# Attention products of different row groups and column halves issued alternately, in separate PSUM banks, in a two-block network on one core

## The chip, the core and the metric

The kernel is one program on one NeuronCore of a Trainium2 chip. What is measured is the device time of one execution, from the first to the last instruction, in microseconds (us). The engines are named as in the profile: PE (TensorE, the matrix products), PEld (its weight loads), DVE (VectorE), ACT (ScalarE), POOL (GpSimd), and SP, whose queue issues the loads from DRAM.

## The reference, cut to what matters

There are 256 tokens of width 1024, all in float32. A first block has a mixer (a dilated attention of 8 heads of 64 beside a retention), a cross attention to a memory, and a mixture of 32 experts. A second block has two layers, each of feed-forward, mixer, feed-forward, and each mixer runs four attentions side by side and one output projection:

```python
def _token_mixers(h, w_in, ...):
    proj = h @ w_in
    a, b, c, d = jnp.split(proj, ...)
    o_a = _mixer_window(a, sink, slopes[:WIN_HEADS])        # 4 heads of 64, 2 key/value heads
    o_b = _mixer_mla(b, ...)                                # 4 heads of 96, values of 64
    o_c = _mixer_axial(c, ax_q_norm, ax_k_norm)             # 4 heads of 64, 2 key/value heads
    o_d = _mixer_diff(d, ...)                               # 4 heads, 2 maps each, of 32
    return jnp.concatenate([o_a, o_b, o_c, o_d], axis=-1) @ w_out

def _dense_attention(q, k, v, scale):
    s = jnp.einsum('bqhgd,bkhd->bhgqk', qi, k).astype(jnp.float32) * scale
    p = jax.nn.softmax(s, axis=-1)
    return jnp.einsum('bhgqk,bkhd->bqhgd', p.astype(v.dtype), v)
```

Scores, softmax over 256 keys and the product with the values are what the change touches. The sums are the same before and after it.

## The kernel before, in words

Every dense product is made exact by splitting both operands into a high and a low part (hi + lo) and issuing three products: hi by hi, hi by lo, lo by hi (`mm3`, lines 308 to 312, so these products all carry the lines L310, L311 and L312). The weights come in chunks of 1 MB through a ring of four tiles, ACT copies the high part (L279), DVE or POOL subtracts the low part (L283).

An attention works on a pair of maps at a time. `scores` (L482) issues six products into one PSUM bank of the tag "mm": 128 tokens by twice 256 keys. Their contraction is short: 64 partitions in the dilated attention and in `gqa` (which computes the axial mixer, called "a", and the window mixer, "w"), 32 in `att_diff` ("d"). Operands of different heads lie on different partitions: the slices in HALVES are rows 0 to 63 and 64 to 127, and `att_diff` has four slices of 32. `softmax` (L429) reads the bank (DVE L437 or L442 for the minimum, ACT L451 for the exponentials), `ptrans` transposes the probabilities in PSUM (L401) and copies them back (ACT L473), and `pv` (L476) multiplies them with the values. An output of `pv` has 64 columns of values, so it takes half of the 128 output partitions; the other head's output goes to the other half of the same bank. These products are plain float32, and each is two matmul instructions in the trace.

Before the change the heads of a pair of halves follow each other: all of half 0 (two token tiles of scores, two softmaxes, transposes, `pv`), then all of half 1. In `att_diff` and the dilated attention the second half's `pv` follows a whole round of scores later; in `gqa` and `att_mla` both column halves are outputs of one call's loop.

PSUM has eight banks, two for each of four tags: "mm" for scores (and the feed-forward's products), "tr" for transposes and `pv`, "a" and "b" for dense accumulators. Inside a mixer of block 2 the dense products use "a" alone, and "b" only serves the last transposes of `att_diff`; the output projection (`dense_sq`, L341) then takes both "a" (token tile 0) and "b" (token tile 1).

The order on each engine is fixed when the program is built: a scheduling pass lays out the instructions by their place in the source and by when their operands and tiles are expected to be free (`schedule_with_timeline_sim=True`), so dense products from further down are put between an attention's steps. Each engine then runs its list strictly in order. Where `pe_order` (L304) is used, the products inside keep the order in which they are written, while others may still come between them. In the mixer of block 2 the source order is MIXERS = "BCHaDdAmw": projections B, C, H, attention a, projection D, attention d, projection A, attentions m and w, then the output projection.

Of the kernel before, what the change touches and what calls it, by code (L numbers as in the profile page):

```python
# [9 lines left out]
F32 = mybir.dt.float32  # L10
# [16 lines left out]
# slots that the dense pools leave free, and those that memory()'s do  # L27
M_EARLY, M_MID = 6, 5

# projections (capitals; H: the heads of B) and attentions of the four mixers in the order of their issue  # L30
MIXERS = "BCHaDdAmw"
OUT = [k for k in MIXERS if k in "adwm"]
# the first gate and up tiles with tokens on partitions; the last down pairs with token tile 0 first, the norm of
# that tile after PLACE of the other's products
NAT, TAIL, PLACE = 2, 3, 4
# products of zeros that bring the tensor engine to its full clock while the first loads arrive
WARM = 18

# ------------------------------------------------------------------ host layout

def _nat(w):
    """[K, N] -> chunks [128, 4 k-tiles, <=512 columns], column groups outermost."""
# [9 lines left out]
def _sq(w, halves=(0, 1)):  # L52
    """[1024, 1024] -> chunks [128, 4 k-tiles, 512 columns], halves of k outermost."""
    n = _nat(w)
    return [n[2 * c + h] for h in halves for c in range(2)]


def _trans(w):
    """[1024, N] -> chunks [128, 2 column tiles, 8 k-tiles, 128 columns]."""
# [55 lines left out]
def _ffn_order():  # L115
    """Gate/up tiles and down pairs in the order of their use."""
# [55 lines left out]
def _pack_moe(i):  # L172
    """Per group of 4 experts: gate and up [k-tile][128, 4, 512], down [half][ff tile][128, 4, 512]."""
# [23 lines left out]
# ------------------------------------------------------------------ program  # L197

class Net:
# [18 lines left out]
    # ---- storage  # L218
# [3 lines left out]
    def turn(s, tags):  # L222
        """The tags of a list in turn."""
        tags.append(tags.pop(0))
        return tags[-1]

    def banks(s):
        """Four accumulators, [token tile][half]."""
# [5 lines left out]
    def bcast(s, pool, name, n, off=0, tag=None, bufs=None, after=None):  # L234
        """A DRAM vector on every partition."""
# [7 lines left out]
    def column(s, pool, name, n, off=0, rep=1):  # L243
        """A DRAM vector down the partitions, rep times."""
# [7 lines left out]
    # ---- weights  # L252
# [12 lines left out]
    def weight(s, width=CH, parts=2, pool=None, own=None, cuts=1):  # L265
        """The next chunk, in parts, each as exact hi + lo, in the ring's tiles, pool's or own."""
# [24 lines left out]
    def own(s, p, i):  # L291
        """Tiles of pool p for a chunk."""
        return [[p.tile([128, CH // 2], F32R, name="own", tag=f"own{j}{k}{i}") for k in range(2)] for j in range(2)]

    def issue_after(s, i, j):
        """i, of the same engine as j, is issued after j."""
# [3 lines left out]
    def plan(s, spec):  # L300
        """Which of the next weight parts get their lo on GpSimd (not d), and after which of the last two powers."""
# [5 lines left out]
    # ---- products  # L307
# [1293 lines left out]
```

## Time and profile before

| | |
|---|---|
| time, median of 3 runs | 1754.07 us (1753.56 to 1755.35) |
| span of the profiled execution | 1753.4 us; the page gives no other time for it, and this is 0.7 us below the median |
| instructions | 24984, of which PE 10070 products and as many weight loads |
| PE busy | 1579.9 us, 90% of the span |
| DVE, ACT, POOL busy | 839.4 us (48%), 657.0 us (37%), 286.9 us (16%) |
| mean granted TensorE clock | 0.941 of full speed |
| dilated attention of block 1 | about 54 to 94 us |
| experts | up to about 722 us |
| attentions of the two mixers of block 2 | about 953 to 1026 us and 1464 to 1537 us |

A busy share is a mean over stages that have different limits: from about 318 us to the end of the experts the chain that ends last runs through the loads, in the rest mostly through PE. What a change in one stage is worth has to be read in that stage. A bar of a matmul in the trace is longer than the step to the next one, because products are pipelined; the step from one start to the next is what it costs.

### The profile page before, as it was taken

Reading aid. Unit: us, or ns where it says so; the run is one execution under the profiler, and the core shown is the slowest. Engines: PE = TensorE matmul, PEld = TensorE weight load, DVE = VectorE, ACT = ScalarE, POOL = GpSimd, SP = SyncE. Lnnn points to the kernel's source line nnn. Section 1 sums busy time; section 2 is a strip of 40 time slices with the busy share of each in tenths; the row PEclk is TensorE's granted clock in tenths of the full one; section 3 lists DMA queues with packets and bytes.
Section 4 is the critical chain, followed back from the end, with each engine's and each line's share of the span. In section 5 each row is a group of like instructions: output and inputs, shape, how many; then the busy total and the mean of one; then the engine's idle time right before and its main releaser. Section 6 shows DMA issues by size and latency. Waiting matters only on the chain.

```text
span 1753.4 us, 24984 instructions
## 1 busy us (share of the span) xinstructions
PE 1579.9 (90%) x10070; PEld 1216.1 (69%) x10070; DVE 839.4 (48%) x1471; ACT 657.0 (37%) x1124; POOL 286.9 (16%) x253
## 2 busy tenths in 40 slices
PE   8999897877667767899999989999999999989998
PEld 6777784322211211599998769999999988779997
DVE  5657653100000000454477675556655667765555
ACT  4655441100000000344435745445444536734442
POOL 4223321100000000222224250000100032340000
PEclk9999998987878877999999989999999999989999
DMA  7444858999999999955554234556355634155552
GB/s 273 142 177 157 327 213 327 419 421 420 421 420 419 421 421 420 368 183 181 190 188 144 97 145 168 192 187 246 143 181 183 240 127 135 49 189 183 181 191 73
DMA packets 66186, 419.06 MB, mean 239 GB/s; under 512 B 10640, under 2 KB 12176, under 8 KB 18704
## 3 DMA queue, kind: packets, MB, share of 16 engines
q1 hardware_dynamic: 66064, 417.39, 62.8%
q8 instruction: 82, 1.34, 0.3%
q14 instruction: 40, 0.33, 0.1%
HBM read 416.32 MB, written 1.05 MB: 238 GB/s over the span
## 4 chain that ended last, share of the span: by engine, by line
PE 55%; DMA 23%; DVE 3%; POOL 1%; issue 1%; ACT 1%; DVEq 0%; SPq 0%; ACTq 0%; POOLq 0%
DMA mraw<-in_wm 23%; PE ps L310 17%; PE ps L312 17%; PE ps L311 17%; PE ps L401 1%; PE ps L480 1%; PE ps L950 1%; DVE xa L1169 1%; PE ps L970 0%; POOL rq L418 0%; PE ps L927 0%; DVE xl L392 0%; DVE lnst L1197 0%; DVE wl L283 0%; POOL ropet L1381 0%
## 5 line engine op out<-in xcount | busy, mean ns | idle before, releaser
L283 DVE TENSOR_TENSOR wl<-raw,wh 128x1024 fp32r<-128x1024 f32 (+2 forms) x314 | 389.3, 1250 | 302.0 <-ACT wh L279 301.1
L279 ACT ACTIVATE wh<-raw 128x1024 fp32r<-128x1024 f32 (+2 forms) x356 | 371.0, 1052 | 351.5 <-PE ps L311 181.1
L310 PE MATMUL ps<-xh,wh 128*128 128x256 f32 x1424 | 402.1, 282 | 3.4 <-ACT cv L1469 3.4
L312 PE MATMUL ps<-xh,wl 128*128 128x256 f32 x1424 | 401.4, 282 | 0.0
L311 PE MATMUL ps<-xl,wh 128*128 128x256 f32 x1424 | 401.0, 282 | 0.0
L310 PEld LDWEIGHTS ps<-xh,wh 128*128 128x128 f32 x1424 | 268.3, 188 | 6.6 <-ACT cv L1469 3.8
L311 PEld LDWEIGHTS ps<-xl,wh 128*128 128x128 f32 x1424 | 268.4, 189 | 1.4
L312 PEld LDWEIGHTS ps<-xh,wl 128*128 128x128 f32 x1424 | 268.4, 188 | 0.8
L950 PE MATMUL ps<-mraw,xg 128*32 128x512 f32 x1024 | 167.7, 758 | 77.4 <-DMA mraw<-in_wm 77.3
L312 PE MATMUL ps<-wh,xl 128*128 128x512 f32 (+3 forms) x520 | 190.1, 370 | 6.5 <-DVE xl L392 6.3
L310 PE MATMUL ps<-wh,xh 128*128 128x512 f32 (+3 forms) x520 | 190.5, 376 | 4.9 <-ACT xh L391 4.1
L311 PE MATMUL ps<-wl,xh 128*128 128x512 f32 (+3 forms) x520 | 191.9, 370 | 2.7 <-POOL wl L283 1.3
L950 PEld LDWEIGHTS ps<-mraw,xg 128*32 128x32 f32 x1024 | 25.6, 119 | 209.0 <-DMA mraw<-in_wm 173.0
L418 POOL TENSOR_TENSOR rq<-rv,mhalf 128x1 f32<-128x1 f32 (+4 forms) x46 | 46.9, 1020 | 728.1 <-DVE rv L416 720.4
L283 POOL TENSOR_TENSOR wl<-raw,wh 128x1024 fp32r<-128x1024 f32 x42 | 103.7, 2473 | 280.9 <-ACT wh L279 263.6
L956 DVE TENSOR_TENSOR mf<-ps,mf 128x512 f32<-128x512 f32 x8 | 5.5, 691 | 248.0 <-PE ps L950 244.1
L312 PEld LDWEIGHTS ps<-wh,xl 128*128 128x128 f32 x520 | 100.6, 194 | 23.2 <-DVE xl L392 10.4
L310 PEld LDWEIGHTS ps<-wh,xh 128*128 128x128 f32 x520 | 100.7, 195 | 22.7 <-ACT xh L391 7.6
L311 PEld LDWEIGHTS ps<-wl,xh 128*128 128x128 f32 x520 | 101.4, 195 | 18.4 <-POOL wl L283 3.4
L311 PE MATMUL ps<-wl,hf 128*128 128x512 f32 x256 | 100.1, 391 | 0.0
L312 PE MATMUL ps<-wh,hf 128*128 128x512 f32 x256 | 100.1, 391 | 0.0
L310 PE MATMUL ps<-wh,hf 128*128 128x512 f32 x256 | 98.2, 390 | 0.0
(357 smaller groups left out, 1981.0 us busy)
## 6 DMA issues: line engine op xcount, KB each, us to landing
mraw<-in_wm SPq DMA_DIRECT2D x191, 1024.0 KB, 19.9
raw<-in_wd SPq DMA_DIRECT2D x179, 1024.0 KB, 4.8
raw<-in_wd SPq DMA_DIRECT2D x8, 512.0 KB, 8.4
raw<-in_wd SPq DMA_DIRECT2D x4, 832.0 KB, 4.7
bc_ln_g<-in_ln_g SPq DMA_DIRECT2D x6, 512.0 KB, 5.7
bc_ln_b<-in_ln_b SPq DMA_DIRECT2D x6, 512.0 KB, 6.5
raw<-in_wd SPq DMA_DIRECT2D x4, 768.0 KB, 4.3
bias<-in_bias SPq DMA_DIRECT2D x4, 512.0 KB, 5.9
```

The source lines that it names most:

```text
L279: s.nc.scalar.activation(h[:, :n], rc, AF.Copy)
L283: i = eng.tensor_tensor(l[:, :n], rc, h[:, :n].bitcast(F32), op=OP.subtract)
L310: mm(out, lhsT=lh, rhs=rh, start=start, stop=False)
L311: mm(out, lhsT=lh, rhs=rl, start=False, stop=False)
L312: mm(out, lhsT=ll, rhs=rh, start=False, stop=stop)
L401: s.nc.tensor.transpose(ps[:, b * 128:b * 128 + 128], src[:, b * 128:b * 128 + 128], s.ident)
L418: s.last_pow = s.nc.gpsimd.tensor_tensor(q, r, s.mhalf[:, :n], op=OP.pow)
L480: s.nc.tensor.matmul(out, lhsT=v(j), rhs=pt[:, 2 * i + j], start=first and j == 0, stop=last and j == 1)
L950: nc.tensor.matmul(ps[32 * e:32 * e + 32], lhsT=xg[:, k, 32 * e:32 * e + 32], rhs=w[:, e * FF:e * FF + FF], start=k == 0, stop=k == NK - 1 ...
L956: nc.vector.tensor_tensor(f, gu[1], f, op=OP.mult)
L1169: nc.vector.scalar_tensor_tensor(z[:, cs], z[:, cs], mv[:, 0:1], g[:, cs], op0=OP.subtract, op1=OP.mult)
```

## The change

`scores` now takes several sets of operands, gives each its own bank, and issues the products of the sets in turn, one of each, in written order (`pe_order`). The sets are two in the dilated attention and `gqa` (both halves of 64 rows) and four in `att_diff` (all slices of 32 rows). `pv` takes pairs of outputs in the two column halves and alternates them in the same way. So both halves of a head pair go through scores, softmax, transposes and `pv` together. The second token tile of `gqa` and two of the four sets of `att_diff` take their banks from the tag "b". The dilated attention issues the loads of both halves' biases at the start of a group; they still share two buffers. `att_diff` copies its output of both halves to SBUF at once. Six instead of four probability tiles are kept (five instead of three in the dilated attention), for which two scratch tiles join the tag "by". The cross attention's products in `memory` are written out in place and stay as they were. Comments are removed throughout; those lines are left out here.

```diff
@@ -419,16 +419,16 @@
-    def softmax(s, pool, ps, bias=None, slope=(1.0, 1.0), sink=None, norm=True, bufs=4):
+    def softmax(s, pool, ps, bias=None, slope=(1.0, 1.0), sink=None, norm=True, bufs=6):
...
@@ -466,32 +466,41 @@
-    def pv(s, out, v, pt, i, first=True, last=True):
-        for j in range(NT):
-            s.nc.tensor.matmul(out, lhsT=v(j), rhs=pt[:, 2 * i + j], start=first and j == 0, stop=last and j == 1)
-
-    def scores(s, q, k):
-        ps = s.bank("mm")
-        for i in range(2):
-            s.mm3(ps[:, i * S:i * S + S], q(i, 0), q(i, 1), k(i, 0), k(i, 1), True, True)
-        return ps
-
+    def pv(s, products):
+        with s.pe_order():
+            for n, pair in enumerate(products):
+                for j in range(NT):
+                    for out, v, pt, i in pair:
+                        s.nc.tensor.matmul(out, lhsT=v(j), rhs=pt[:, 2 * i + j], start=n + j == 0,
+                                           stop=n == len(products) - 1 and j == 1)
+    def scores(s, maps, tags=("mm", "mm")):
+        banks = [s.bank(t) for t in tags[:len(maps)]]
+        with s.pe_order():
+            for i in range(2):
+                for a, b in ((0, 0), (0, 1), (1, 0)):
+                    for (q, k), ps in zip(maps, banks):
+                        s.nc.tensor.matmul(ps[:, i * S:i * S + S], lhsT=q(i, a), rhs=k(i, b), start=a + b == 0,
+                                           stop=a == 1)
+        return banks
...
@@ -590,19 +599,20 @@
+            bias = [p.tile([128, 2, 2, S], F32, name="bias", tag="bias", bufs=2) for _ in HALVES]
+            for e in range(2):
+                nc.sync.dma_start(bias[e], a["bias1"][:, 4 * g + 2 * e:4 * g + 2 * e + 2])
+            probs = [], []
+            for t in range(NT):
+                tk = slice(t * 128, t * 128 + 128)
+                banks = s.scores([(lambda i, j, r=r: qt[j][r, 2 * g + i, tk], lambda i, j, r=r: kt[j][r, 2 * g + i])
+                                  for r in HALVES])
+                for e in range(2):
+                    probs[e].append(s.softmax(p, banks[e], [bias[e][:, i, t] for i in range(2)], bufs=5))
+            pt = [s.ptrans(p, probs[e]) for e in range(2)]
             po = s.bank("b")
-            for e, r in enumerate(HALVES):
-                bias = p.tile([128, 2, 2, S], F32, name="bias", tag="bias", bufs=2)
-                nc.sync.dma_start(bias, a["bias1"][:, 4 * g + 2 * e:4 * g + 2 * e + 2])
-                probs = []
-                for t in range(NT):
-                    tk = slice(t * 128, t * 128 + 128)
-                    ps = s.scores(lambda i, j: qt[j][r, 2 * g + i, tk], lambda i, j: kt[j][r, 2 * g + i])
-                    probs.append(s.softmax(p, ps, [bias[:, i, t] for i in range(2)], bufs=3))
-                pt = s.ptrans(p, probs)
-                for i in range(2):
-                    h = 4 * g + 2 * i + e
-                    s.pv(po[r, i * S:i * S + S], lambda j: va[:, j, h * 64:h * 64 + 64], pt, i, i == 0, i == 1)
+            s.pv([[(po[r, i * S:i * S + S], lambda j, h=4 * g + 2 * i + e: va[:, j, h * 64:h * 64 + 64], pt[e], i)
+                   for e, r in enumerate(HALVES)] for i in range(2)])
...
@@ -780,7 +790,9 @@
-                        s.pv(po[:, :S], lambda j: s.mv[:, j, k * 128:k * 128 + 128], pt, e)
+                        for j in range(NT):
+                            nc.tensor.matmul(po[:, :S], lhsT=s.mv[:, j, k * 128:k * 128 + 128], rhs=pt[:, 2 * e + j],
+                                             start=j == 0, stop=j == 1)
...
@@ -1416,7 +1428,7 @@
-            y = q.tile([128, 4, 96], F32, name="my", tag="my", bufs=2)
+            y = q.tile([128, 4, 96], F32, name="my", tag="by", bufs=2)
...
@@ -1427,14 +1439,14 @@
-            y = q.tile([128, 4, 96], F32, name="my", tag="my", bufs=2)
+            y = q.tile([128, 4, 96], F32, name="my", tag="by", bufs=2)
...
@@ -1470,21 +1482,22 @@
-        for e, r in enumerate(HALVES):
-            probs = []
-            for t in range(NT):
-                tk = slice(t * 128, t * 128 + 128)
-                ps = s.scores(lambda i, j: qt[j][r, i, tk], lambda i, j: kt[j][r])
+        probs = [], []
+        for t in range(NT):
+            tk = slice(t * 128, t * 128 + 128)
+            banks = s.scores([(lambda i, j, r=r: qt[j][r, i, tk], lambda i, j, r=r: kt[j][r]) for r in HALVES],
+                             ("b", "b") if t else ("mm", "mm"))
+            for e, ps in enumerate(banks):
                 if bias is None:
-                    probs.append(s.softmax(q, ps))
+                    probs[e].append(s.softmax(q, ps))
                 else:
-                    probs.append(s.softmax(q, ps, [bias[:, t]] * 2, (0.5 ** (2 * e + 1), 0.5 ** (2 * e + 2)),
-                                           sink[:, 2 * e:2 * e + 2]))
-            pt = s.ptrans(q, probs)
+                    probs[e].append(s.softmax(q, ps, [bias[:, t]] * 2, (0.5 ** (2 * e + 1), 0.5 ** (2 * e + 2)),
+                                              sink[:, 2 * e:2 * e + 2]))
+        for e in range(2):
+            pt = s.ptrans(q, probs[e])
             po = s.bank("tr")
-            for i in range(2):
-                s.pv(po[HALVES[i], :S], lambda j: v[:, j, e * 64:e * 64 + 64], pt, i)
+            s.pv([[(po[HALVES[i], :S], lambda j: v[:, j, e * 64:e * 64 + 64], pt, i) for i in range(2)]])
...
@@ -1501,23 +1514,25 @@
-            for e, r in enumerate(HALVES):
-                s.pv(po[r, :S], lambda j: mv[:, j, (2 * g + e) * 64:(2 * g + e) * 64 + 64], pt, e)
+            s.pv([[(po[r, :S], lambda j, h=2 * g + e: mv[:, j, h * 64:h * 64 + 64], pt, e)
+                   for e, r in enumerate(HALVES)]])
...
-        for e, r in enumerate(HALVES):
-            probs = []
-            for t in range(NT):
-                tk = slice(t * 128, t * 128 + 128)
+        probs = [], []
+        for t in range(NT):
+            tk = slice(t * 128, t * 128 + 128)
+            rows = [slice(32 * n, 32 * n + 32) for n in range(4)]
+            banks = s.scores([(lambda g, j, r=r: dq[j][r, g, tk], lambda g, j, r=r: dk[j][r, g]) for r in rows],
+                             ("mm", "mm", "b", "b"))
+            for e in range(2):
...
-                    ri = slice(64 * e + 32 * i, 64 * e + 32 * i + 32)
-                    ps = s.scores(lambda g, j: dq[j][ri, g, tk], lambda g, j: dk[j][ri, g])
-                    x, y = s.softmax(q, ps, [m["far"][:, 0, t]] * 2, (0.5 ** (5 + e), 0.5 ** (7 + e)), norm=False)
+                    x, y = s.softmax(q, banks[2 * e + i], [m["far"][:, 0, t]] * 2, (0.5 ** (5 + e), 0.5 ** (7 + e)),
+                                     norm=False)
...
@@ -1527,18 +1542,17 @@
-                probs.append(pr[0])
-            pt = s.ptrans(q, probs)
-            po = s.bank("tr")
-            for g in range(2):
-                s.pv(po[r, g * S:g * S + S], lambda j: dv[:, j, (2 * g + e) * 64:(2 * g + e) * 64 + 64], pt, g,
-                     g == 0, g == 1)
-            nc.scalar.activation(oT[r].rearrange("p g c -> p (g c)"), po[r], AF.Copy)
+                probs[e].append(pr[0])
+        pt = [s.ptrans(q, probs[e]) for e in range(2)]
+        po = s.bank("tr")
+        s.pv([[(po[r, g * S:g * S + S], lambda j, h=2 * g + e: dv[:, j, h * 64:h * 64 + 64], pt[e], g)
+               for e, r in enumerate(HALVES)] for g in range(2)])
+        nc.scalar.activation(oT.rearrange("p g c -> p (g c)"), po, AF.Copy)
...
-            y = q.tile([128, 256], F32, name="dy", tag="dy")
+            y = q.tile([128, 256], F32, name="dy", tag="by", bufs=2)
...
```

## Rows read from the trace of the kernel before

**Rows 1.** Windows by stage: length, busy us (count) of PE, PEld, DVE, ACT, POOL, clock.

```profile
50.00:95.00 45.00, 43.55 (x254) 33.26 (x253) 24.76 (x74) 26.46 (x59) 8.43 (x4) 1.00 0.50 176
955.00:995.00 40.00, 40.00 (x259) 33.15 (x258) 28.36 (x84) 28.34 (x78) 8.38 (x8) 1.00 0.38 132
995.00:1010.00 15.00, 13.86 (x95) 10.08 (x93) 9.64 (x36) 10.96 (x36) 2.20 (x3) 1.00 0.00 1
...
955.00:1026.00 71.00, 69.37 (x433) 54.67 (x432) 50.00 (x151) 49.98 (x137) 17.49 (x14) 1.00 0.26 92
1466.00:1537.00 71.00, 69.38 (x434) 54.78 (x432) 50.09 (x151) 50.15 (x137) 17.49 (x14) 1.00 0.26 91
```

**Rows 2.** Timeline of PE around one call of scores: start, length, what.

```profile
54.03 0.39 PE L311 MATMUL ps<-wl,xh 128*128 128x512 f32 x1
54.26 0.39 PE L312 MATMUL ps<-wh,xl 128*128 128x512 f32 x1
54.57 0.38 PE L310 MATMUL ps<-kt,qt 64*128 64x256 f32 x1
54.80 0.28 PE L311 MATMUL ps<-kt,qt 64*128 64x256 f32 x1
54.91 0.28 PE L312 MATMUL ps<-kt,qt 64*128 64x256 f32 x1
...
55.48 0.39 PE L310 MATMUL ps<-xh,wh 128*128 128x256 f32 x1
55.70 0.29 PE L311 MATMUL ps<-xl,wh 128*128 128x256 f32 x1
```

**Rows 3.** Timeline of PE where two calls of scores meet.

```profile
62.47 0.39 PE L310 MATMUL ps<-kt,qt 64*128 64x256 f32 x2
62.69 0.28 PE L311 MATMUL ps<-kt,qt 64*128 64x256 f32 x2
62.82 0.28 PE L312 MATMUL ps<-kt,qt 64*128 64x256 f32 x1
```

**Rows 4.** Groups of PE's products by line and shape: count, busy us, mean ns.

```profile
L950 PE MATMUL ps<-mraw,xg 128*32 128x512 f32 x1024 | 167.7, 758 | 77.4 <-DMA mraw<-in_wm 77.3 <-DVE xg L928 0.2
...
L310 PE MATMUL ps<-dk,dq 32*128 32x256 f32 x32 | 10.5, 329 | 0.0
...
L480 PE MATMUL ps<-pt,dv 128*64 128x256 f32 x32 | 7.8, 385 | 0.0
L480 PE MATMUL ps<-pt,va 128*64 128x256 f32 x32 | 7.8, 385 | 0.0
...
L480 PE MATMUL ps<-pt,cv 128*64 128x256 f32 x32 | 4.4, 392 | 0.0
```

**Rows 5.** Timeline of PE: one step of the experts' products.

```profile
302.87 0.64 PE L950 MATMUL ps<-mraw,xg 128*32 128x512 f32 x4
```

**Rows 6.** Timeline of PE: one call of pv in the dilated attention.

```profile
74.28 1.94 PE L480 MATMUL ps<-pt,va 128*64 128x256 f32 x8
76.15 0.38 PE L310 MATMUL ps<-kt,qt 64*128 64x256 f32 x1
```

**Rows 7.** Timeline of PE: first and last of eight calls of scores in att_diff.

```profile
967.86 0.38 PE L310 MATMUL ps<-dk,dq 32*128 32x256 f32 x1
...
989.38 0.38 PE L310 MATMUL ps<-dk,dq 32*128 32x256 f32 x1
```

**Rows 8.** Timeline of PE: the dense products on both sides of a stretch without any.

```profile
992.44 0.40 PE L312 MATMUL ps<-wh,xl 128*128 128x512 f32 x1
...
1010.42 0.48 PE L310 MATMUL ps<-wh,xh 128*128 128x512 f32 x1
```

**Rows 9.** Timeline of POOL: one combination of two maps in att_diff, two instructions.

```profile
993.05 1.83 POOL L1527 TENSOR_SCALAR pr<-pr,lr 128x256 f32<-128x256 f32 x2 [4.20 <-DVE lr L1524]
```

**Rows 10.** The chain that ended last, in order of time, through the experts: first and last of 20 such pieces.

```profile
318.02 19.76 DMA mraw<-in_wm
...
701.17 17.50 DMA mraw<-in_wm
```

## Prediction

> **What bounds the kernel now.** I first read the windows by stage, because the change touches three short stretches and a mean over the span says little about them. In the dilated attention of block 1 PE is busy 43.55 of 45 us, while DVE and ACT are busy 24.8 and 26.5 us; in the attentions of a mixer of block 2 PE is busy 69.4 of 71 us, DVE and ACT 50.0 each, and the second layer repeats the first to 0.1 us [rows 1]. The clock is full in all of them. So PE sets the pace there, and a microsecond taken from it counts, until a softmax on DVE and ACT ends later than the products that were laid beside it.
>
> The chain that ended last agrees where it matters: it runs through PE outside the experts, and through the loads in them, 20 pieces of about 20 us from 318 us on [rows 10]. These loads run without a break once they are behind, so an earlier block 1 starts that train earlier and what it gains isn't lost there.
>
> Next comes the timeline of PE, to see what one call of `scores` costs. Dense products of 512 columns start 0.23 us apart; to the first score product it is 0.31 (+0.08), then 0.23 to the second and 0.11 to the third; from the first score product to the next dense one it is 0.91, and that one needs 0.22 to its successor where 0.12 is usual (+0.10) [rows 2]. So six products cost 0.91 + 0.08 + 0.10 = 1.09 us, of which 6 x 0.12 = 0.72 is products and 0.37 is the going in and out of the short shape.
>
> **Do different row groups run together here?** The trace of before has a place by accident, where two calls of different halves meet: two products start within 0.01 us and their joint bar is 0.39, that of one alone 0.38 [rows 2, 3]; the next two have a joint bar of 0.28, that of one alone, and 0.13 later the next starts [rows 3]. So a pair costs what one costs. For column groups the experts show four at once: four products in 0.64 us, where the mean bar of one is 0.758 [rows 4, 5]. And `pv` shows both cases: 32 instructions of one shape are busy 4.4 us for cv but 7.8 us for dv and va [rows 4]. In `gqa` (and `att_mla`, whose group reads the same) the two column halves already alternate, so `pv` gains nothing there; only the dilated attention and `att_diff` have their halves in separate calls, one after the other.
>
> **The change part by part.**
> Scores of the dilated attention: 8 calls of 6 become 4 of 12, in pairs. A call of six pairs takes as long as one of six products, so 4 x 1.09 = 4.4 us go.
> Its `pv`: one call of 8 instructions takes 76.15 - 74.28 = 1.87 us [rows 6]. Four become two of 16, which in pairs take as long as one did: 2 x 1.87 = 3.7 us go.
> `gqa`, called for a and w: per layer 8 calls become 4, 4.4 us.
> `att_diff`: 8 calls become 2 of 24. If four row groups run like two, six calls go: 6.5 us. Four row groups at once are not in this trace; if only two ran together, a call would take 0.37 + 12 x 0.125 = 1.87, and the gain is 8 x 1.09 - 2 x 1.87 = 5.0. I take 6.5, because four column groups do run together [rows 5].
> The Trainium skill (TensorE: Matmul & The Clock Gate, Part 3: Packing small matmuls) gives a measured 3.07 for four row tiles of 32, not 4. By that a call of 24 products would hold 24 x 0.12 / 3.07 = 0.94 us of products in place of 0.72, an estimate of 0.9 us more over the four calls; no row here shows it.
> Its `pv`: two calls become one, 1.9 us per layer.
> The sum is 8.1 us in block 1 and 4.4 + 6.5 + 1.9 = 12.8 us per layer, 33.7 us in all, if all PE time saved were time saved.
>
> What is added costs little by itself. The copy of `att_diff`'s output on ACT becomes one instead of two. The bias loads of the dilated attention's second group wait longer: both buffers are held until the second token tile of the first group is read; behind them in SP's queue stand the weights. I price this at nothing as long as PE has the retention's dense products between, and at up to 2 us, a fraction of the 8.1, if not. Shared scratch tiles and more probability tiles only relax waits, or follow uses long past.
>
> The new waits are on banks. A call's products are in written order over two or four banks, so the first that lacks its bank holds the call. `att_diff`'s second call needs all four banks of its first, so four softmaxes have to be read. In before the eight calls are spread from 967.86 to 989.38, 3.1 us apart [rows 7]; at that pace four softmaxes are 12 us. Other products can stand in between: projection A has 72 products at 0.12, 8.6 us, but later there is little. From 992.44 to 1010.42 before has no dense product at all, since the output projection waits for `att_diff` [rows 8], and PE is already idle 1.1 of 15 us there [rows 1].
>
> **How much of it arrives.** Block 1: PE's idle share is small, DVE and ACT have 40% to spare and dense products follow, so I take 0.8 of 8.1: 6.5 us. Layer, up to 995: a and d lose 2.2 + 6.5 = 8.7 us of 40. DVE and ACT, busy 28.4 us each, would then be at 91% of the 31.3 us left, which I don't expect of steps that wait for each other; at 84% the stretch is 33.9 us, so 6.1 us are saved, 0.7 of 8.7. After 995: 1.9 of `pv` and 2.2 of w, with nothing dense to fill; I take half, 2.0. That is 8.1 per layer. The sum: 6.5 + 2 x 8.1 = 22.7 us off the span of 1753.4, 1730.7, and 0.7 for the median over it: 1731 us. The factors 0.8, 0.84 and a half are chosen between nothing and all.
>
> **Rivals.**
> All of it arrives: the steps of DVE and ACT move forward with PE. 33.7 us, 1720. For it: nothing but PE is above 71% in these stretches. Against it: the 91% above. 0.17.
> Softmax becomes the bound: the products are quick, but banks are emptied no faster, and the copies of `ptrans`, the POOL step of 1.83 us for each of the four combinations of `att_diff` [rows 9] and the exponentials stand in line. Then perhaps 0.3 of the layers' 25.6 and 0.6 of block 1's 8.1 arrive: 12.5 us, 1742. The Trainium skill (TensorEngine Tiling (Array Packing), PSUM Bottleneck) says the same of tiling in general, that emptying PSUM may take over as the limit. 0.25.
> The products don't run together in written order, or others are put between them so that pairs are torn: then only fewer goings in and out remain, 4 + 2 x 10 calls at 0.37, 8.9 us, of which some 5 arrive, 1749; if the calls are torn as well, no change. Against it: rows 3. 0.06.
> Slower: the bank waits are not covered. The place is `att_diff`, then m and w behind it. Up to 12 us for each of its two calls stand against 12.8 us saved per layer, so it decides from 12.8 us of uncovered wait. With 16 us uncovered per layer the layers lose 2 x 3.2, block 1 still gains some 2 us: 1758. Against it: the order is made knowing of these waits, and projection A can stand in. 0.08.
> My forecast, between 1724 and 1737, has 0.44.
>
> **How the numbers follow.** 1731 is the likeliest case. The range leaves out the outer part of the first rival and the slower case: 1718 to 1748. A difference of 0.2%, 3.5 us, is about what a measurement can tell from no change. Faster by more: 0.17 + 0.44 + 0.25 - 0.02 for the weak end + 0.03 of the torn case = 0.87; I say 0.86. Within it: 0.05. Slower: 0.09.
>
> **What would show it.** In the profile after: score products in bars of two (dilated, `gqa`) and of four (`att_diff`) with one step of about 0.12 for all of them; `pv` of dv and va near 4.4 us as cv; calls of 12 and 24 about 0.9 us long; the stretch from the first score of a to the end of w's `pv` some 8 us shorter in each layer, the dilated attention 6 us. The prediction is wrong if the groups of four take two steps, if PE shows waits of several us for DVE or ACT between calls, or if the idle time reappears before the output projection.

## The result and the profile after

The changed kernel takes 1765.04 us (median of 4 runs, 1762.15 to 1767.24) against 1753.82 us beside it, a ratio of 1.006 with a 95% interval of 1.0046 to 1.0074: slower by 0.6%, where 1731 us was forecast. The profiled execution is the fastest of the four, 1762.15 us, with a span of 1760.5 us.

The first reading is where the time went. The table compares the starts of stages in the two traces; "norm" is the first transpose of the normed tokens ahead of a mixer (layer 0) or behind it.

| stage starts at, us | before | after | difference |
|---|---|---|---|
| last `pv` of the dilated attention | 93.7 | 88.6 | -5.1 |
| norm ahead of layer 0's mixer | 908.1 | 900.7 | -7.4 |
| norm behind it | 1038.5 | 1038.1 | -0.5 |
| norm ahead of layer 1's mixer | 1418.9 | 1419.0 | +0.1 |
| norm behind it | 1549.7 | 1556.8 | +7.1 |

Up to the first mixer 7.4 us are gained, about what was forecast, and the loads of the experts pass it on. This is one execution of each kernel: over the traces of all kernels below, which share this part, the norm ahead of layer 0 lies anywhere between 898.7 and 904.7 us. The mixers then lose 6.9 and 7.0 us. So the question lies in the mixers.

The windows by stage show what is missing there (columns as in [rows 1]; the last lines of the group split the second stretch):

```profile
50.00:95.00 45.00, 41.55 (x281) 32.84 (x280) 27.61 (x76) 29.32 (x68) 8.22 (x4) 1.00 0.50 176
...
980.00:995.00 15.00, 10.07 (x51) 7.52 (x52) 10.52 (x38) 9.65 (x34) 3.64 (x4) 0.66 0.00 1
995.00:1010.00 15.00, 11.93 (x86) 8.23 (x83) 8.22 (x36) 8.47 (x26) 6.13 (x5) 1.00 0.00 0
...
980.00:985.00 5.00, 2.02 (x12) 1.55 (x12) 3.26 (x15) 3.28 (x12) 1.57 (x2) 0.78 0.00 0
985.00:990.00 5.00, 3.06 (x13) 2.68 (x14) 3.99 (x15) 3.38 (x11) 2.08 (x3) 0.50 0.00 0
```

Before, PE was busy without a break up to 995 us, 87 us after the norm, at a clock of 1.00 [rows 1]. Now it is busy 10.07 of 15 us from 980 us (79 us after the norm), and 2.02 of 5 us in its first third; the granted clock falls to 0.50, the 1.2 GHz level, so that part of that busy time is slow work. No other engine is full either: DVE is busy 10.52 of the 15 us, ACT 9.65.

The chain that ended last shows what sets the time in this stretch. In before it runs on PE alone from 955 us until this piece:

```profile
995.83 0.69 DVE mn L437
```

In after it leaves PE at 972.77 us, and up to 988.88 us only six transposes of PE are in it. First come the parts of a weight (L279), then `att_diff`'s softmaxes, one behind the other: exponentials on ACT (L451), the combination of two maps on POOL (L1542) and DVE:

```profile
972.56 0.13 PE ps L311
972.77 1.07 ACT wh L279
...
976.25 1.11 ACT pr L451 x4
...
978.00 0.93 POOL pr L1542
...
981.69 1.10 ACT pr L451 x4
...
983.43 0.93 POOL pr L1542
...
985.23 1.53 PE ps L401 x6
...
988.88 0.58 PE ps L310
```

So for 16 us the order of these steps is the bound, though none of their engines is full.

The groups of PE's products by line and shape answer [rows 4]:

```profile
L494 PE MATMUL ps<-dk,dq 32*128 32x256 f32 x96 | 8.2, 312 | 0.0
...
L483 PE MATMUL ps<-pt,dv 128*64 128x256 f32 x32 | 6.1, 421 | 0.0
...
L483 PE MATMUL ps<-pt,va 128*64 128x256 f32 x32 | 5.2, 389 | 0.0
...
L483 PE MATMUL ps<-pt,cv 128*64 128x256 f32 x32 | 4.3, 392 | 0.0
```

The timeline of PE shows both that the products run together and what happens to the calls:

```profile
54.41 0.97 PE L494 MATMUL ps<-kt,qt 64*128 64x256 f32 x12
55.32 0.39 PE L310 MATMUL ps<-xh,wh 128*128 128x256 f32 x1
...
944.42 0.38 PE L494 MATMUL ps<-ck,cq 64*128 64x256 f32 x2
...
945.49 0.97 PE L494 MATMUL ps<-ck,cq 64*128 64x256 f32 x11
...
949.49 0.39 PE L494 MATMUL ps<-ck,cq 64*128 64x256 f32 x2
...
950.38 0.86 PE L494 MATMUL ps<-ck,cq 64*128 64x256 f32 x9
...
958.39 0.39 PE L494 MATMUL ps<-dk,dq 32*128 32x256 f32 x2
...
960.44 0.38 PE L494 MATMUL ps<-dk,dq 32*128 32x256 f32 x1
...
964.83 0.86 PE L494 MATMUL ps<-dk,dq 32*128 32x256 f32 x18
...
977.45 0.96 PE L494 MATMUL ps<-dk,dq 32*128 32x256 f32 x21
...
978.53 0.71 PE L312 MATMUL ps<-wh,xl 128*128 128x512 f32 x2
...
996.29 0.97 PE L494 MATMUL ps<-wk,wq 64*128 64x256 f32 x11
...
1003.94 0.48 PE L310 MATMUL ps<-wh,xh 128*128 128x512 f32 x1
...
1008.14 0.97 PE L494 MATMUL ps<-wk,wq 64*128 64x256 f32 x11 [0.62 <-DVE xl L392]
```

Twelve products in pairs take 0.97 us with the last bar, and the next dense product starts 0.91 us after the first of them, as it did after six [rows 2]; 21 in fours take 0.96 us with the last bar. But `att_diff`'s first call is torn: two products at 958.39, a third at 960.44, the rest at 964.83 us. w's second call comes 11.9 us after its first and waits for DVE's `xl`, the last step of `att_diff`'s tail, which uses the tag "b". And the dense products stop with the two at 978.53 us, of which the second starts at 978.85, and start again at 1003.94 us: 25.1 us from start to start, where it was 18.0 before [rows 8].

The start of a needs the list of PE as it was built, since the trace leaves out buffer numbers. Banks 7344 and 7345 ("mm") are the first token tile's, 7381 and 7382 ("b") the second's; products of one kind in a row are joined here:

```
L494 7381, 7382 in turn               x2
...
L494 7381, 7382 in turn               x10
L494 7344                             x1   waits for ACT
...  11 dense products, 4 transposes, 5 dense products
L494 7345                             x1   waits for ACT
L494 7344                             x1
...  4 transposes
L494 7345, 7344 in turn               x9
```

The call at 944.42 and 945.49 us is that of the second tile, whose softmaxes come last. The first tile's call needs both banks of "mm", and H's head products still hold them: one product enters the first bank, and nothing more can follow until the second bank is free (ACT's last read of it, L1446, ends at 946.74 us) and its place in the list comes. The first softmax of a is read at 951.73 us, 0.5 us after the last bar of that call ends (950.38 + 0.86). In the timeline of DVE:

```profile
948.23 0.96 DVE L283 TENSOR_TENSOR wl<-raw,wh 128x768 fp32r<-128x768 f32 x1 [1.32 <-ACT wh L279]
949.11 0.41 DVE L392 TENSOR_TENSOR dk<-ps,dk 128x256 fp32r<-128x256 f32 x1
949.44 0.68 DVE L395 SCALAR_TENSOR_TENSOR mq<-ps,mq 96x512 fp32r<-96x512 f32 x1
951.12 0.69 DVE L392 TENSOR_TENSOR mk<-ps,mk 96x512 fp32r<-96x512 f32 x1 [1.00 <-ACT mk L391]
951.73 0.68 DVE L437 TENSOR_REDUCE mn<-ps 128x2 f32<-128x512 f32 x1
```

Four other operations stand ahead of the read in DVE's list. That leaves two readings of the late start: the products came late, or the list held the read. In this trace the list can account for 0.5 us at most. The last two experiments part them.

### The profile page after: what moved, and what is told of

Read it like the earlier page. It is cut to its first block, busy times and chain, and to the rows that moved or that the text cites. A ratio compares the mean times of both kernels' runs of the same rounds, so it can differ in the third digit from the quotient of the medians.

```text
span 1760.5 us, 24970 instructions
## 1 busy us (share of the span) xinstructions
PE 1566.3 (89%) x10070; PEld 1203.1 (68%) x10070; DVE 839.5 (48%) x1471; ACT 656.1 (37%) x1122; POOL 285.1 (16%) x253
## 3 DMA queue, kind: packets, MB, share of 16 engines
q1 hardware_dynamic: 66064, 417.39, 62.6%
## 4 chain that ended last, share of the span: by engine, by line
PE 53%; DMA 24%; DVE 3%; ACT 2%; POOL 1%; issue 1%; SPq 0%; DVEq 0%; POOLq 0%; ACTq 0%
DMA mraw<-in_wm 23%; PE ps L310 16%; PE ps L312 16%; PE ps L311 16%; PE ps L401 2%; PE ps L483 1%; PE ps L494 1%; DVE xa L1181 1%; ACT pr L451 1%; DVE wl L283 0%; ACT pt L473 0%; PE ps L962 0%; ACT wh L279 0%; DVE xl L392 0%; POOL rq L418 0%
## 5 line engine op out<-in xcount | busy, mean ns | idle before, releaser
L279 ACT ACTIVATE wh<-raw 128x1024 fp32r<-128x1024 f32 (+2 forms) x356 | 371.0, 1052 | 349.0 <-PE ps L311 179.1
```

The costliest lines, as they stand in the source:

```text
L279: s.nc.scalar.activation(h[:, :n], rc, AF.Copy)
```

## The experiments

Intervals of the ratios to before are about 0.1% to each side, 2 us, so a difference between two of these kernels is uncertain by about 3 us, an estimate from two such intervals. Each kernel computes all that the reference asks.

**Which part loses.** Three kernels undo parts of the change: all of the mixers, `att_diff` alone, `gqa` alone. A fourth keeps every bank and every softmax in its order, and only takes the alternation out of the mixers' scores (the halves of `att_diff`'s `pv` still alternate):

```
-            for i in range(2):
-                for a, b in ((0, 0), (0, 1), (1, 0)):
-                    for (q, k), ps in zip(maps, banks):
...
+            for m in [zip(maps, banks)] if alt else [[n] for n in zip(maps, banks)]:
+                m = list(m)
+                for i in range(2):
+                    for a, b in ((0, 0), (0, 1), (1, 0)):
+                        for (q, k), ps in m:
```

> Only the dilated attention of block 1 is changed; the four mixers of both layers are as before the change. If block 1's gain of about 7.6 us is real and the loss of 6.9 us per layer belongs to the mixers alone, the time is 1753.8 - 7.6 = 1746 us. If part of the gain only exists because the layers move (or the loss comes from block 1's other timing), it ends within 3 us of 1754.

Measured: 1748.61 us, ratio 0.997 (0.9959 to 0.9981). Block 1's change alone is a gain of 6.1 us.

> As after, but att_diff in its old form (eight calls of six products, one bank each, its pv in two calls); the regrouped gqa and the dilated attention stay. Theory (att_diff's calls over four banks tear, bunch its softmaxes and use up the dense products early): the layers lose little or nothing, about 1746 us or a few us less. Rival (gqa's regrouping, its bank b for the second token tile, is to blame): the loss stays, 1757 to 1765 us.

> As after, but gqa in its old form (four calls of six products, on one pair of banks, half by half); att_diff stays in calls of 24 over four banks. Theory (att_diff is to blame): the loss stays nearly whole, 1757 to 1765 us. Rival (gqa's regrouping is to blame): about 1740 to 1746 us.

Measured: 1758.39 us with the old `att_diff`, 1755.01 us with the old `gqa`. Both parts lose, 6.6 and 10.0 us, and the sum of 16.6 us is what lies between after and the first run (16.4). My first theory, `att_diff` alone, fell.

> As after in every bank, call and order of softmaxes, but inside each call of gqa and att_diff the products of one bank are written whole before those of the next, so no two row groups alternate in the mixers (they still do in block 1). If the loss comes from the alternation tying several banks together (one bank not free holds all), this is faster than after although PE does up to 10.9 us more work per layer: below 1760 us. If the loss comes from the regrouping itself (token tile outermost: the transposes of a half wait for three or more softmaxes, and both halves' pv come last), the loss stays, and PE's extra work adds to it: 1765 us or more.

Measured: 1753.38 us, 11.7 us less than after, though PE has more to do. So most of the loss is the alternation's. The regrouping loses too: against the run with the mixers in their old form (1748.61 us) this one is 4.8 us slower, and 11.7 and 4.8 make up the 16.4 us.

**Which wait.** Four runs change one bank or one size. The first edit puts w's second call on "mm", once in after and once in the kernel that writes bank after bank (where `alt=False` stands behind it); the second puts a's and w's there; the third makes pairs of `att_diff`'s fours:

```
-                             ("b", "b") if t else ("mm", "mm"))
+                             ("b", "b") if t and sink is None else ("mm", "mm"))
...
-                             ("b", "b") if t else ("mm", "mm"))
+                             ("mm", "mm"))
...
-                             ("mm", "mm", "b", "b"))
             for e in range(2):
+                banks = s.scores([(lambda g, j, r=r: dq[j][r, g, tk], lambda g, j, r=r: dk[j][r, g])
+                                  for r in rows[2 * e:2 * e + 2]], ("b", "b") if e else ("mm", "mm"))
...
```

> As after, but the second call of w takes its banks from mm, as its first, and not from b (a keeps b). New theory: in after w's last softmax starts 111.1 us after the norm ahead of the mixer begins, 106.9 before the change, because w's second call waits for the banks b behind att_diff's tail; of the 6.9 us lost per layer this is about 4.2. Then 1765 - 2 x 4.2 = 1757 us (1754 to 1760), and w's second pair of softmaxes starts some 7 us after the first pair in place of 11.8. Rival (the bank is only where the wait shows, the call would wait for the softmaxes on DVE anyway): 1762 to 1767 us.

> The run of bank after bank (1753.4 us) with w's second call on mm instead of b. There w's second pair of softmaxes also starts 11.5 us after the first. If b is the cause, 3 to 4 us per layer come back here too: 1746 us (1743 to 1749), and the softmax of w that is last starts near 104 us after the norm. Rival (without alternation the call was not held by b): no change, 1752 to 1755 us.

Measured: 1759.14 and 1749.51 us, 5.9 and 3.9 us less than without this edit, where 8 and 7 were expected. In the profile of the first, w's two calls stand at 997.61 and 1003.58 us, 6.0 apart in place of 11.9, so the wait on "b" is gone:

```profile
992.96 3.67 PE L483 MATMUL ps<-pt,dv 128*64 128x256 f32 x14
997.61 1.04 PE L494 MATMUL ps<-wk,wq 64*128 64x256 f32 x11
...
1003.58 0.97 PE L494 MATMUL ps<-wk,wq 64*128 64x256 f32 x11
```

But w's first call comes later too, so that in layer 0 its last softmax is read 111.5 us after the norm, no earlier than in after (111.1), and the mixer is 1.4 us shorter; in layer 1 these are 109.2 against 111.5, and 4.0 us. With bank after bank the mechanism is as expected: 104.3 in place of 107.7 us.

> As after, but att_diff's scores in four calls of 12 over two banks each (the two maps of one half together, the first half in mm, the second in b), in the same order of softmaxes. Undoing all of att_diff gave 1758.4, 6.6 us less than after. If that part of the loss comes from one call holding four banks, this gives it back: about 1759 us. Rival (it comes from the regrouping, both halves' pv at the end): 1763 to 1766 us.

Measured: 1759.36 us, 5.7 us less, so in this kernel a call over four banks is nearly the whole of what `att_diff` lost. The runs of this kernel spread widely, from 1752.5 to 1764.8 us.

> As after, with both calls of both gqa on mm, so that b belongs to att_diff alone until its tail. Over the run with w alone on mm it moves a: its second call has to wait for the first two softmaxes, but att_diff's first call no longer waits for a's last two. Theory: w's 8 us come back as there, and att_diff's first call of 24 is not torn; together 1750 to 1757 us. Rival (a's second call now comes late, and all behind it): no better than the run with w alone, 1757 us or more.

Measured: 1760.10 us, no better than with w alone on "mm"; a's second call then comes after 54 more dense products in PE's list, and a's four softmaxes take 13.2 us from first to last read in place of 6.5.

**Precedence in the written order.** The scores and all softmaxes were put in a block of higher priority for the scheduling pass.

> All scores alternate as in after, with att_diff in pairs and w's second call on mm, and in addition the products of gqa's and att_diff's scores and every softmax take precedence over other work when the order on each engine is written. Without the precedence the two earlier runs add up to 1765 - 5.7 - 5.9 = 1753 us. Theory (alternating costs because a softmax is read behind other operations that the written order puts ahead of it, a's first 5 us late): the first softmax of a starts 46 to 47 us after the norm, as before the change, and the time is 1745 to 1750 us. Rival (alternated calls cost by holding two banks until the end, whatever the order): 1752 to 1757 us, with the softmax of w that is last no earlier than 107 us.

> The run with no alternation in the mixers (bank after bank, w on mm, 1749.5 us), with precedence for scores and softmaxes as in the run of all pairs. PE's list then has 4 to 16 dense products between the calls of six of att_diff, down to the last. If it is the filler (dense products left for the late softmaxes) that sets the mixer's length, this is faster than 1749.5: 1742 to 1747 us, with no window of 5 us below 80% PE before m. If not, 1749 to 1753 us.

> As the run with pairs in att_diff alone, with precedence for scores and softmaxes. PE has about 4 x 1.1 us per layer less to do than in the run of bank after bank with precedence, and dense products still stand between the calls. If time follows PE once the order feeds the softmaxes, 2 to 4 us below that run per layer at most, 1738 to 1745 us; if the softmaxes set the pace, the same as that run within 2 us.

Measured: 1755.18, 1751.51 and 1750.15 us. Each time the outcome that I thought likelier, given first, didn't come. The last two without precedence take 1749.51 (bank after bank) and 1742.76 us (next), so for pairs it costs 7.4 us; the first has no counterpart without precedence. In the first run a's first softmax is still read 51.4 us after the norm.

**The part that pays.**

> Alternation in block 1 and in att_diff (in pairs) only; gqa writes its calls bank after bank, and w's second call is on mm. Between the run with no alternation in the mixers (1749.5 us) and after. If pairs in att_diff cost nothing and give PE's time back, 1746 to 1749 us; if any alternation in a mixer costs, some 3 us above 1749.5: 1752 to 1755 us.

Measured: 1742.76 us (1741.43 to 1744.26), ratio 0.9936 (0.9923 to 0.9948), faster than before and after, and 5.9 us faster than block 1's change alone; I call it the best version. The PE timeline of it shows a's second tile and the first bank of the first tile run in one go (12 and 6 products, the first of them earlier), `att_diff`'s calls whole, and a dense gap of 18.8 us:

```profile
946.47 0.38 PE L496 MATMUL ps<-ck,cq 64*128 64x256 f32 x1
...
947.65 1.57 PE L496 MATMUL ps<-ck,cq 64*128 64x256 f32 x17
...
968.82 0.97 PE L496 MATMUL ps<-dk,dq 32*128 32x256 f32 x11
...
974.73 0.97 PE L496 MATMUL ps<-dk,dq 32*128 32x256 f32 x11
...
982.62 0.40 PE L312 MATMUL ps<-wh,xl 128*128 128x512 f32 x1
...
1001.44 0.48 PE L310 MATMUL ps<-wh,xh 128*128 128x512 f32 x1
```

The windows of the same kernel, at the place of the two windows of 15 us above (its norm is 2.1 us later), show PE fed and the clock nearly full. Here the chain that ended last runs on PE from 970 to 983.69 us, and ACT has 1.59 us of it before it is back on PE at 985.83:

```profile
982.00:997.00 15.00, 13.07 (x84) 9.40 (x83) 9.12 (x33) 10.21 (x34) 2.86 (x3) 0.89 0.20 69
997.00:1012.00 15.00, 14.25 (x78) 10.82 (x75) 11.92 (x41) 11.11 (x30) 8.03 (x5) 1.00 0.00 1
```

**One edit at a time from there.**

> The fastest version so far (1742.8 us: att_diff in pairs, gqa bank after bank, w's second call on mm), with a's two calls alternating again and w's not. In after a's first bank is complete 5.3 us before it is read, because DVE's list has four other operations ahead. Theory (a's late start carries through the whole row of softmaxes and moves dense products ahead of it): a's first softmax at 51 in place of 46.5 us after the norm, 4 to 5 us lost per layer, 1750 to 1753 us. Rival (a has time to spare, w at the end is what counts): 1742 to 1745 us.

> The fastest version so far, with w's two calls alternating again (on mm) and a's not. Behind w there is only the output projection. Theory (a's late start is the main loss; at w's place the pairs only save 2 x 1.1 us of PE per layer or cost a late read): 1742 to 1748 us. Rival (w at the end is what counts): 1750 us or more.

> The fastest version so far, with att_diff's calls of 24 over four banks as in after in place of pairs. PE has two goings in and out and six steps per call less to do. If a call that holds four banks loses by itself (5.7 us between after and the run of pairs), 1746 to 1750 us. If it only lost together with gqa's late start, 1738 to 1743 us.

> Block 1 as after, att_diff in pairs, and gqa in its form of before the change (half by half, one pair of banks). If the regrouping of gqa by token tile with four banks for a pays (a's four softmaxes read within 8.6 us in place of 12.2), this is slower than 1742.8: 1746 to 1749 us. If it is indifferent, 1742 to 1745 us.

Measured: a alternating 1751.95 us (+9.2), w alternating 1742.01 us (-0.8, no difference), four banks in `att_diff` 1749.79 us (+7.0), `gqa` as before the change 1754.81 us (+12.0, more than expected). Alternation at w costs nothing once its banks are "mm". The expectation of the first took the second tile's call for the first tile's: what was complete 5.3 us ahead of the read was not the bank that is read.

The last of these runs limits all that was said of `att_diff`. With the old `gqa`, pairs (1754.81) and fours (1755.01, above) take the same time, and both are some 6 us slower than the old `att_diff` with the old `gqa` (1748.61). So neither the price of four banks nor the gain of pairs holds by itself: both were measured beside the regrouped `gqa`, and with the old one there is no price to see and no gain.

With four banks `att_diff`'s second call is torn again, three products of their own and then the rest, 8.3 us after the first:

```profile
967.89 0.38 PE L496 MATMUL ps<-dk,dq 32*128 32x256 f32 x1
...
969.69 0.38 PE L496 MATMUL ps<-dk,dq 32*128 32x256 f32 x1
...
972.06 0.38 PE L496 MATMUL ps<-dk,dq 32*128 32x256 f32 x1
...
976.20 0.97 PE L496 MATMUL ps<-dk,dq 32*128 32x256 f32 x21
```

**Why a loses.** The operations that stood ahead of the read in DVE's list are bound behind it, or, with no alternation in a, the read is bound behind them:

```
+            for i in s.behind:
+                s.issue_after(i, r)
...
+                s.issue_after(j, s.first)
```

Here r and `s.first` are the first read of a, `s.behind` holds the last splits of mq and mk, and j is the last split of dk; the last part of D's weight is bound likewise. In the second run the two arguments change places.

> As the run with a alternating again (1751.9 us), but the four operations of DVE that stood ahead of the first softmax's read of a are bound to come behind it (two last splits of H, one of D, one weight part). Theory (the place of the read in DVE's list is the cost, not the alternation): a's first softmax is read some 46 to 47 us after the norm, and the time is 1741 to 1746 us. Rival (the alternation itself costs): 1750 us or more.

> As the fast version with a bank after bank (1742.8 us), but the first softmax's read of a is bound to come behind the same four operations of DVE. Nothing else is changed, a's products do not alternate. Theory (the place of the read is the cost): a's first softmax is read near 51 us after the norm and the time is 1749 to 1754 us. Rival (a late start of a is made up for, the alternation itself costs): 1742 to 1745 us.

Measured: 1746.17 and 1752.34 us. The second is as the theory had it: with a's products one bank after another, a late read alone costs 9.6 us in the median. The first came in the right direction for another reason. The read was put first and still came 50.4 us after the norm, because its products weren't there: DVE stood idle 4.26 us for them. Its PE and DVE timelines:

```profile
951.68 0.39 PE L506 MATMUL ps<-ck,cq 64*128 64x256 f32 x2
...
952.58 0.86 PE L506 MATMUL ps<-ck,cq 64*128 64x256 f32 x9
```

```profile
953.37 0.69 DVE L442 TENSOR_REDUCE mn<-ps 128x2 f32<-128x512 f32 x1 [4.26 <-PE ps L506]
```

So DVE's list isn't the cause of the late start in the kernels that alternate at a; the tied products are.

The positions of the softmaxes' reads in layer 0, in us after the norm ahead of the mixer, taken from the starts in the traces (in brackets the median of the kernel; the last two profiled executions took 1751.0 and 1746.3 us):

| kernel | a, first | d, first to last | w, last | norm behind the mixer |
|---|---|---|---|---|
| before | 46.0 | 61.3 to 82.8 | 106.8 | 130.4 |
| after | 51.0 | 65.0 to 84.3 | 111.1 | 137.3 |
| pairs in d only (1742.8) | 46.5 | 60.9 to 78.9 | 103.6 | 128.1 |
| and a alternating (1752.0) | 51.0 | 61.0 to 81.3 | 104.3 | 132.3 |
| and four banks in d (1749.8) | 46.5 | 62.3 to 80.8 | 105.2 | 131.3 |
| a alternating, read first (1746.2) | 50.4 | 62.6 to 81.2 | 106.8 | 131.4 |
| a bank after bank, read late (1752.3) | 50.8 | 62.2 to 81.3 | 103.5 | 130.2 |

What the late start leads to isn't what the expectations say. By w's last read it is made up for: 104.3 and 103.5 us with a late, against 103.6. What is lost in layer 0 comes behind that read: 28.0 and 26.7 us to the norm, against 24.5.

## Why the prediction was wrong

**The cost of a call: right.** A call of 12 takes 0.91 us from its first product to the next dense one, as one of six did. Calls of 24 in fours take one step for each four as well, so the bound of two steps for four row groups, and with it 5.0 instead of 6.5 us, is excluded. By the Trainium skill's 3.07 (TensorE: Matmul & The Clock Gate, Part 3: Packing small matmuls) a call would have been longer by an estimated 0.22 us; the four starts lie within 0.01 us of each other, and from the second four on the next come 0.11 to 0.12 us later, as for a pair, so this trace doesn't show the loss.

**`pv`: right in mechanism.** The groups fell from 7.8 to 5.2 us (va) and 6.1 us (dv), not to 4.4. In the dilated attention the call is 14 products in 1.94 us behind a first pair of 0.65 us.

**Block 1: right.** 6.5 us were forecast, the run of it alone gave 6.1. The bias loads cost nothing to be seen. The factor 0.8 in it was chosen, so that the two come this close is partly luck.

**The step that failed is "How much of it arrives", with its rival "Slower: the bank waits are not covered".** The layers were to gain 8.1 us each and lost 6.9 and 7.0, 30 us in both, most of the 34 us of error; the profiled execution, from which these are taken, is 2.9 us below the median. The sum counts PE time saved and has no term for the waits on banks. The rival that names them had the place right, but its price and its chance (0.08) were wrong.

First, I counted a wait on banks only from 12.8 us upwards, against PE time saved, as if dense products would fill it. They filled it, and were then missing: projection A's last product starts 71.8 us after the norm, where it was 79.4 before, and the twelve products of the output projection that can go ahead are used up at 78.1 us, where it was 84.3. Behind them PE had only what the softmaxes gave it, and 25.1 us pass without a dense product where 18.0 did [rows 8]. That is the condition of the prediction's first paragraph, that a softmax ends later than the products that were laid beside it; the chain that ended last leaves PE there for 16 us.

Second, "the order is made knowing of these waits" was no argument: the three waits stand in the order as built. They are a's pair tied to H's banks (9.2 us in both layers, against the best version), w's second call on "b" behind `att_diff`'s tail (5.9 us, against after), and the call over four banks (5.7 us against after, 7.0 against the best version). The sum of 20.8 to 22.1 us is close to the 22.3 us between after and the best version, but the three are measured from two different kernels and the third vanishes beside the old `gqa`, so this is no proof that they add up.

**The rival "softmax becomes the bound": right in its mechanism, wrong in its time.** DVE and ACT are not above 80% and 68% in the poor windows of after, which says little, since a chain of steps on three engines fills none of them. The steps that this rival names, the exponentials, POOL's combination and the copies of `ptrans`, do stand in line in the chain that ended last, from 972.77 to 988.88 us. It was to leave a gain of 12.5 us; it came together with the waits on banks, and there was a loss. By the Trainium skill (TensorEngine Tiling (Array Packing), PSUM Bottleneck) the emptying of PSUM may take over; this trace shows a chain of which the reads of PSUM are one step, and no engine that empties banks at its limit.

**All of it arrives: no.** Even the best version gains 11.4 us (1754.2 to 1742.8), a third of the 33.7 us.

What stays open: by what path a's alternation costs 9.2 us. The late read alone costs as much (9.6 us), yet with the alternation and the read put first the start was as late and the time only 3.4 us above the best, and in layer 0 the late start is made up for by w's last read. Each of these edits gives every engine another list, so what belongs to the start and what to the lists behind it isn't parted. It isn't shown either why `att_diff` in pairs gains beside the regrouped `gqa` and loses beside the old one, or why higher precedence for the scores made the best version 7.4 us slower.

## What to carry to other kernels

Products of different row groups that alternate in written order finish their banks together: the call can't go on before the last of its banks is free, and no softmax gets its bank before the end of the call. So alternate only as many as there are banks free at that moment, never with a tag that another step still holds, and try a call at the start of a chain bank after bank as well. In the best version that meant pairs in `att_diff`, not fours, and no pairs at a; beside another form of `gqa` pairs and fours were the same, so measure such choices together. And price a wait that dense products can fill by where those products would otherwise have stood: here they were used up 6 us earlier, and what followed was a chain of softmaxes with nothing beside it. Busy shares don't show such a bound; the chain that ended last does.

## What was not expected of the hardware

The clock makes idle time dear. In after PE was busy 2.02 of 5 us from 980 us; the granted clock, 1.00 in the 5 us before, was 0.78 in the mean of these and 0.50 in the next. In the run with w on "mm" 14 products of dv's `pv` took 3.67 us in such a stretch, against 1.94 us in after, where the clock was back. Some of these kernels also vary more: the 12 runs of pairs in `att_diff` with a alternating and w on "b" lie between 1752.5 and 1764.8 us, the 5 of the best version between 1741.4 and 1744.3. That the clock is the cause of this isn't shown.
